# ScalarE instead of VectorE reads the banks of the queries' transposed sums and of the samples' indexer products

## The chip, the core and the metric

The kernel runs on one core of a Trainium2 chip. The metric is the device time of one execution in microseconds, the median of several executions. The core's engines are TensorE (PE), VectorE (DVE), ScalarE (ACT), GpSimd (POOL) and SyncE (SP, which issues most DMAs).

## The reference

One inference step of a decoder layer, for a prompt of 1024 tokens and 8 samples that each add one token to 1024 cached ones, with 1024 features, all in fp32:

```
h    = rms_norm(x) * (1 + scale) + shift          # from the condition c
q, k, v, qi, ki, wi, ga, u, gp = split(h @ w_in)
q, k = rms_norm per head of 64                    # 8 heads, 2 for keys
score = sum over 8 heads of wi * relu(qi . ki)    # the indexer
attend over the 256 tokens of highest score       # per query, causal
p_out = pooled windows (2, 4, 8, 16) of u, times w_pool
y = x + gate * (concat(a_out * silu(ga), p_out * silu(gp)) @ w_out)
```

Two pieces of it matter here. The samples' indexer: for each of the 8 samples the scores of 1024 cached tokens are `sum over heads of wi * relu(qi . ki)`, and the 256 best of 1025 are kept. And the RMS norm of the queries, which needs the sum of squares of every head of every token.

## The kernel before, in words

Each fp32 product is made of three matmuls of fp32r halves, an upper and a lower part of both factors (`hh`, `hl` for the activations, `wh_`, `wl_` for a block of weights). ACT makes the upper part of a weight block (L293), POOL the lower one (L297).

The program has one long stretch in which PE projects blocks of `w_in` one after the other. In the part of interest, from about 200 to 330 us, these are u1, u2, gp0, u3, gp1, q0, gp2, q1, q2 and on, each in three chunks of 344 columns and eight steps of the contraction. In this part the order on PE, DVE and ACT is that in which the program is written. All the smaller work is written as generators that stand in named queues (`beside`); `project` (L514) emits six matmuls, about one microsecond of PE, and then calls `tick`, which lets each queue go on by its rate. So a step that lies one tick later stands six projection matmuls later in PE's order, and behind whatever else the other queues emit in that tick.

`sample_indexer` (L879) is such a generator. For each sample b `pipeline` runs the stages load (POOL's indirect DMA of cached keys, `kin`), turn (PE, L912, `pkin`), copy (ACT, L916, `kidT`), dot (PE, L922, `p_ix`), copy_x (DVE, L927, `sx`), back (PE, L931, `p_ixT`), weigh (DVE, L936 and L939): offsets in ticks of 0, 5, 6, 9, 11, 15 and 16, and a new sample every 4 ticks. The banks of `p_ixT`, of the pooling's products `ppo` (L1223) and of the queries' sums `pqs` and `pqt` are two, in rotation (tag "sm"); `p_ix`, `pkin`, `p_row` and others alternate in two more. A bank is written again once its reader is done.

The weighted sums of heads land in `s_sc`. `sample_search` (L964) then turns them into rows with PE (L973, `p_row`), DVE copies the rows (L975, `s_row`), computes their spread, POOL makes the steps of a bisection from it, and ACT does eight halvings (L734 to L736). In the same stretch `topk` looks for the thresholds of the prompt's blocks: counts by DVE (L764) and ACT (L734), and per halving three small steps of DVE on 128x4: `tk_keep`, `tk_d`, `tk_t` (L768, L770, L772). Later DVE takes the largest (L799) and replaces them (L806); a branch on `tk_bad` (L830), for DVE alone, skips more rounds, and `sample_masks` follows (L1006, L1007, PE's `p_smask` L1011).

For a group of queries `take_q` (L1248) squares the projections on ACT. Its generator `norms` (L1252) sums the squares per head with PE, transposes the sums into the bank `pqt`, DVE copies 16 and 8 of their columns into `qss` (L1266, L1267), and `rstd_steps` forms the reciprocal root: `ms` (DVE, L252), the power `y` (POOL, L253), three steps of DVE (L255 to L257). The pooling's own work on POOL stands in the same queue of POOL as `y`: window sums (L1199), `pdl` (L1215), `sgp` (L1228) and the weights' lower parts.

Of the kernel before, what the change touches and what calls it, by code (L numbers as in the profile page):

```python
# [8 lines left out]
F32 = mybir.dt.float32  # L9
# [20 lines left out]
IXP = 4  # L30
IXB = 15
# [5 lines left out]
AF = mybir.ActivationFunctionType  # L37
ALU = mybir.AluOpType
# [3 lines left out]
P = 128  # L42
# [4 lines left out]
B = 8  # L47
# [9 lines left out]
NPAGES = 8  # L57
CHUNKS = ((0, 344), (344, 344), (688, 344))
QCHUNKS = ((256, 388), (644, 388))
HEADS = 8  # L60
# [5 lines left out]
def kernel(  # L66
# [8 lines left out]
    nc = tc.nc  # L75
# [25 lines left out]
    small = ctx.enter_context(tc.tile_pool(name="small", bufs=2))  # L101
# [5 lines left out]
    def row(name, dt=F32, n=N):  # L107
        return rows.tile([P, n], dt, tag="row", name=name)

    def t2k(name):  # L110
        return work.tile([P, 512], F32, tag="t2k", name=name, bufs=3)

    def s2k(name):
        return work.tile([P, 512], F32, tag="s2k", name=name, bufs=2)

    def page_tile(name, n):
        return work.tile([P, n], F32, tag="pg", name=name, bufs=2)
# [4 lines left out]
    def ps_small(name, shape=(P, 512), dt=F32):  # L122
        return pss.tile(list(shape), dt, tag="sm", name=name)
# [3 lines left out]
    def ps_one(name, shape=(P, 512), dt=F32, tag="sb"):  # L127
        return pss.tile(list(shape), dt, tag=tag, name=name, bufs=1)

    def ps_side(name, shape=(P, 512), dt=F32):  # L130
        side[0] ^= 1
        return ps_one(name, shape, dt, ("sa", "sb")[side[0]])

    def ps_two(name, shape=(P, 512), dt=F32):
        return pss.tile(list(shape), dt, tag="sm", name=name)
# [19 lines left out]
    def beside(queue, gen, rate):  # L155
        queues.setdefault(queue, {"gens": [], "acc": 0.0})["gens"].append((gen, rate))
# [24 lines left out]
    def lag(n):  # L181
        for _ in range(n):
            yield

    def pipeline(n, period, *stages):

        for t in range((n - 1) * period + max(o for o, _ in stages) + 1):
            for o, f in sorted(stages, key=lambda x: -x[0]):
                i, r = divmod(t - o, period)
                if r == 0 and 0 <= i < n:  # L190
                    f(i)
            yield
# [186 lines left out]
    ssq = const.tile([P, NB], F32, name="ssq")  # L379
# [13 lines left out]
    def spread(half, pr):  # L393

        for i in range(4):
            mm(pr[:, i * P:(i + 1) * P], rstd[:, 4 * half + i:4 * half + i + 1].to_broadcast([P, P]), ident,
               start=True, stop=True)
        return scale_rows[:, half * 512:half * 512 + 512], pr
# [52 lines left out]
    to, pr = spread(0, ps_one("pr0", tag="sb"))  # L451
# [23 lines left out]
    to, pr = spread(1, ps_small("pr1"))  # L475
# [395 lines left out]
    def load_pages(dst, src, b):  # L871
        nc.gpsimd.indirect_dma_start(out=dst, out_offset=None, in_=src,
                                     in_offset=bass.IndirectOffsetOnAxis(ap=pidx[:, b:b + 1], axis=0))
# [5 lines left out]
    def sample_indexer():  # L879
        wis_bd = const.tile([B, B, HEADS], F32, name="wis_bd")  # L880
        nc.vector.tensor_tensor(wis_bd, ident[0:B, 0:B].unsqueeze(2).to_broadcast([B, B, HEADS]),
                                wi_s.unsqueeze(1).to_broadcast([B, B, HEADS]), op=ALU.mult)
        pw = ps_side("pwsb", (P, 64))
        mm(pw, ones_f[0:B, :], wis_bd.rearrange("p a b -> p (a b)"), start=True, stop=True)
        yield
        wsb = const.tile([P, 64], F32, name="wsb")
        nc.vector.tensor_copy(wsb, pw)
        nc.vector.memset(s_sc[:, 8, :], NEG)
        yield
        p_ixn = ps_side("p_ixn", (B, B, HEADS))  # L890
        mm(p_ixn.rearrange("p (a o) h -> p a (o h)", o=2), ki_sT, qibd[0:64, :, 0].rearrange("p a o h -> p a (o h)"), start=True, stop=True)
        yield
        rxn = const.tile([B, 64], F32, name="rxn")
        nc.vector.scalar_tensor_tensor(rxn, p_ixn.rearrange("p b h -> p (b h)"), 0.0, wsb[0:B, :],
                                       op0=ALU.max, op1=ALU.mult)
        nc.vector.tensor_reduce(out=s_sc[0:B, 8, :], in_=rxn.rearrange("p (b h) -> p b h", h=HEADS), axis=AX.X,
                                op=ALU.add)
        yield
        nc.gpsimd.affine_select(out=s_sc[0:B, 8, :], in_=s_sc[0:B, 8, :], pattern=[[1, B]],
                                compare_op=ALU.is_equal, fill=NEG, base=0, channel_multiplier=-1)  # L900
        kin, pk, kidT, px, sx, rx = {}, {}, {}, {}, {}, {}

        def load(b):
            if b % 2 == 0:
                kin[b] = page_tile(f"kin{b}", S)
                kin[b + 1] = kin[b][:, 512:S]
            load_pages(kin[b][:, 0:512], rows_ki, b)

        def turn(b):
            pk[b] = ps_side(f"pkin{b}", (P, 4, P))  # L910
            for i in range(4):
                nc.tensor.transpose(pk[b][:, i, :], kin[b][:, i * P:(i + 1) * P], ident)  # L912

        def copy(b):
            kidT[b] = s2k(f"kidT{b}").rearrange("p (g d) -> p g d", d=P)
            nc.scalar.copy(kidT[b], pk[b])  # L916

        def dot(b):

            px[b] = ps_side(f"p_ix{b}", (P, P))  # L920
            for i in range(4):
                mm(px[b][32 * i:32 * i + 32, :], qibd[:, b // 2].rearrange("p g o h -> p (g o h)"), kidT[b][:, i, :],  # L922
                   start=True, stop=True)

        def copy_x(b):
            sx[b] = s2k(f"sx{b}")[:, 0:P]
            nc.vector.tensor_copy(sx[b], px[b])  # L927

        def back(b):
            pt = ps_two(f"p_ixT{b}", (P, NPAGES, 2, HEADS))  # L930
            nc.tensor.transpose(pt.rearrange("p t o h -> p (t o h)"), sx[b], ident)  # L931
            px[b] = pt[:, :, b % 2, :]

        def weigh(b):
            rx[b] = small.tile([P, NPAGES, HEADS], F32, tag="s_rx", name=f"rx{b}")
            nc.vector.scalar_tensor_tensor(  # L936
                rx[b], px[b], 0.0, wsb[:, b * HEADS:(b + 1) * HEADS].unsqueeze(1).to_broadcast([P, NPAGES, HEADS]),
                op0=ALU.max, op1=ALU.mult)
            nc.vector.tensor_reduce(out=s_sc[:, 0:8, b], in_=rx[b], axis=AX.X, op=ALU.add)  # L939

        yield from pipeline(B, IXP, (0, load), (5, turn), (6, copy), (9, dot), (11, copy_x), (IXB, back), (IXB + 1, weigh))


    s_row = {}
# [300 lines left out]
    def take_q(j):  # L1245
        qp[j] = row(f"qp{j}")
        sq = row(f"qsq{j}")

        def norms():
            yield from lag(2)  # L1250

            pq = ps_two(f"pqs{j}", (P, 2, P))  # L1252
            for b in range(NB):
                g, i = divmod(b, 4)
                mm(pq[32 * i:32 * i + 32, g, :], blk[:, 48:80], sq[:, b * P:(b + 1) * P], start=True, stop=True)
            yield
            qs = t2k(f"qs{j}")[:, 0:2 * P].rearrange("p (g t) -> p g t", t=P)
            nc.scalar.copy(qs, pq)
            yield from lag(QLAG)
            pr = ps_two(f"pqt{j}", (P, 24, 16))  # L1260
            for g in range(2):
                nc.tensor.transpose(pr[:, 8 * g:8 * g + 8, :].rearrange("p a b -> p (a b)"), qs[:, g, :], ident)
            mm(pr[:, 16, 0:8], blk, sq[:, S:N], start=True, stop=True)
            yield
            ssq = small.tile([P, 24], F32, tag="qss", name=f"qss{j}", bufs=1)
            nc.vector.tensor_copy(ssq[:, 0:16], pr[:, 0:16, 0])  # L1266
            nc.vector.tensor_copy(ssq[:, 16:24], pr[:, 16, 0:8])  # L1267
            rs = small.tile([P, 24], F32, tag="qrs", name=f"qrs{j}")
            yield from rstd_steps(rs, ssq, 64)
            nc.vector.tensor_scalar(rq8[:, j].rearrange("p a b -> p (a b)"), rs[:, 0:16], 0.125, None, op0=ALU.mult)  # L1270
            nc.vector.tensor_tensor(qbd[0:64, :, j], qp[j][0:64, S:N], rs[0:64, 16:24], op=ALU.mult)
            nc.vector.tensor_tensor(qbd[64:128, :, 4 + j], qp[j][64:128, S:N], rs[64:128, 16:24], op=ALU.mult)

        def take(ci, c0, n, pt):
            nc.scalar.activation(qp[j][:, c0:c0 + n], pt, AF.Copy, scale=qnw)
            nc.scalar.activation(sq[:, c0:c0 + n], pt, AF.Square)
            if ci == 2:
                beside("prep", norms(), 1.0)
        return take
# [490 lines left out]
```

## Time and profile before

| what | value |
|---|---|
| median of 3 runs | 626.29 us (624.5 to 626.4) |
| the profiled execution, its own time | 625.83 us |
| its span in the profile | 624.1 us |
| mean granted clock of PE | 0.997 |
| PE busy | 596.9 us, 96% of the span |
| DVE busy | 386.9 us, 62% |
| ACT busy | 306.7 us, 49% |
| POOL busy | 238.5 us, 38% |

A row of the timeline is an instruction: its start in us, its length in us, engine, line of the program, operation, what it writes and reads (names without their numbers), shapes, and, in brackets, how long its engine had been idle before and what ended that. Where an engine is never idle for long, as PE here, its waits are what can be taken away. A wait of a matmul for a reader of its bank is listed with that reader's engine and line.

### The profile page before, as it was taken

To read this page: it belongs to the slowest core of one execution; us is meant where nothing else is said; L and a number is where in the kernel's file an instruction comes from. 1 tells how busy PE (TensorE), PEld (TensorE's weight loads), DVE (VectorE), ACT (ScalarE), POOL (GpSimd) and SP (SyncE) were. 2 spreads that over 40 slices of the span, in tenths; PEclk is the share of its full clock that TensorE was granted. 3 is DMA by queue.
4 is the path that set the end of the run, shared out by engine and by line. 5 is a ranking of instruction groups with operands and counts; after the bars stand their busy time and mean duration, and the time that the engine had idled before them with its cause. 6 is when DMAs were issued, how large, how long until landed. Compare 5 with 4: busy or idle time off the path is not lost. (4 is left out here: it accounts for less than half of the span.)

```text
span 624.1 us, 10765 instructions
## 1 busy us (share of the span) xinstructions
PE 596.9 (96%) x4086; PEld 492.8 (79%) x4086; DVE 386.9 (62%) x900; ACT 306.7 (49%) x570; POOL 238.5 (38%) x226
## 2 busy tenths in 40 slices
PE   4899999999989998999989999999999999999997
PEld 4678999999979998998868886565666566878876
DVE  4797468647465889959965047555687665464242
ACT  5633554545456885681422458655777554102000
POOL 3111346111247468475816873303544043006000
PEclk9999999999999999999999999999999999999999
DMA  8994122330427123023264243212121136066231
GB/s 307 289 291 102 52 46 76 95 91 19 116 63 222 35 81 90 1 73 79 51 176 136 85 154 136 102 35 69 35 68 35 30 108 227 12 181 206 90 102 67
DMA packets 75290, 66.02 MB, mean 106 GB/s; under 512 B 21828, under 2 KB 63900, under 8 KB 75229
## 3 DMA queue, kind: packets, MB, share of 16 engines
q1 hardware_dynamic: 69731, 50.57, 28.4%
q0 software_dynamic: 3008, 10.49, 5.6%
q10 hardware_dynamic: 2498, 4.27, 1.8%
q8 instruction: 32, 0.52, 0.3%
q14 instruction: 21, 0.17, 0.1%
HBM read 54.44 MB, written 11.10 MB: 105 GB/s over the span
## 5 line engine op out<-in xcount | busy, mean ns | idle before, releaser
L1591 ACT ACTIVATE pr<-pr,mx,rq 128x128 f32<-128x128 f32 (+7 forms) x64 | 55.4, 866 | 12.3 <-DVE mx L1589 11.8
L677 DVE SCALAR_TENSOR_TENSOR sc<-r,wtok,sc 128x512 f32<-128x512 f32 (+5 forms) x42 | 45.1, 1082 | 25.9 <-ACT r L670 24.8
L670 ACT ACTIVATE r<-pi 128x512 f32<-128x512 f32 (+5 forms) x48 | 36.3, 759 | 49.0 <-PE pi L668 43.4
L1619 PE MATMUL po<-pTs,v_sb 128*64 128x256 f32 (+1 forms) x320 | 52.6, 381 | 0.0
L1703 PE MATMUL py<-woh,mh 128*128 128x512 f32 (+1 forms) x136 | 52.1, 383 | 0.0
L1703 PE MATMUL py<-woh,ml 128*128 128x512 f32 (+1 forms) x136 | 51.8, 381 | 0.0
L1703 PE MATMUL py<-wol,mh 128*128 128x512 f32 (+1 forms) x136 | 51.8, 381 | 0.0
L1603 PE MATMUL pT<-ident,pr 128*128 128x128 f32 x288 | 48.8, 283 | 0.1
L1585 DVE CUSTOM_DVE_ANT_0 pr<-pl,amask 128x384 f32<-128x384 f32 (+5 forms) x48 | 42.1, 886 | 9.3 <-PE pl L1582 8.9
L1603 PEld LDWEIGHTS pT<-ident,pr 128*128 128x128 f32 x288 | 32.5, 141 | 17.5 <-issue 15.6
L145 ACT COPY pTs<-pT 128x512 f32<-128x512 f32 x40 | 23.2, 581 | 33.6 <-PE pT L1603 33.6
L1723 DVE TENSOR_TENSOR y<-py,gate_p 128x512 f32<-128x512 f32 (+1 forms) x17 | 11.2, 657 | 42.4 <-PE py L1703 42.4
L1446 POOL TENSOR_TENSOR wol<-wo,woh 128x1024 fp32r<-128x1024 f32 x8 | 19.5, 2444 | 36.6 <-ACT woh L1445 30.3
L147 DVE COPY pTs<-pT 128x512 f32<-128x512 f32 (+1 forms) x40 | 23.3, 582 | 15.1 <-PE pT L1603 11.7
L514 PE MATMUL pj_u<-hh,wh_u 128*128 128x344 f32 x96 | 32.5, 339 | 0.1
L514 PE MATMUL pj_q<-hh,wh_q 128*128 128x344 f32 x96 | 31.8, 331 | 0.0
L514 PE MATMUL pj_gp<-hh,wh_gp 128*128 128x344 f32 x96 | 31.7, 330 | 0.0
L1619 PEld LDWEIGHTS po<-pTs,v_sb 128*64 128x64 f32 x320 | 18.0, 135 | 17.4 <-issue 9.4
L514 PE MATMUL pj_q<-hh,wl_q 128*128 128x344 f32 x96 | 30.8, 321 | 0.5 <-POOL wl_q L297 0.5
L514 PE MATMUL pj_ga<-hh,wh_ga 128*128 128x344 f32 x96 | 31.2, 325 | 0.0
L1703 PEld LDWEIGHTS py<-woh,mh 128*128 128x128 f32 x136 | 25.6, 188 | 6.9 <-DVE y L1724 0.8
L514 PE MATMUL pj_ga<-hh,wl_ga 128*128 128x344 f32 x96 | 30.8, 320 | 0.0
(449 smaller groups left out, 1754.2 us busy)
## 6 DMA issues: line engine op xcount, KB each, us to landing
ada<-in_w_ada_dram SPq DMA_DIRECT2D x16, 512.0 KB
x<-in_x_prompt_dram SPq DMA_DIRECT2D x8, 512.0 KB
gate<-in_w_ada_dram SPq DMA_DIRECT2D x8, 512.0 KB
mix<-mix_dram SPq DMA_DIRECT2D x8, 512.0 KB
xr<-in_x_prompt_dram SPq DMA_DIRECT2D x15, 256.0 KB
out_dram<-y ACTq DMA_DIRECT2D x15, 256.0 KB
mix_dram<-sga SPq DMA_DIRECT2D x12, 172.0 KB
mix_dram<-sgp SPq DMA_DIRECT2D x12, 172.0 KB
```

The costliest lines, as they stand in the source:

```text
L145: nc.scalar.copy(out, in_)
L147: nc.vector.tensor_copy(out, in_)
L514: mm(pt[:m, :n], wt[:, k, :m], ht[k][:, c0:c0 + n], start=k == 0 and q == 0, stop=k == KT - 1 and q == 2)
L670: nc.scalar.activation(r[:, 0:L].rearrange("p (c n) -> p c n", c=nh), pt[:, 0:nh, :n], AF.Relu)
L677: nc.vector.scalar_tensor_tensor(sb[:, 0:L], r[:, 0:L], wtok[:, b, h:h + 1], sb[:, 0:L], op0=ALU.mult, op1=ALU.add)
L1446: nc.gpsimd.tensor_tensor(lo, t, hi.bitcast(F32), op=ALU.subtract)
L1585: nc.vector.tensor_tensor_reduce(out=pr[:, 0:L].rearrange("p (c n) -> p c n", c=nh), in0=pt[:, 0:nh, :n], in1=amask[b].rearrange("p (c n) ...
L1591: exps.append(lambda: nc.scalar.activation(pr[:, 0:L], pr[:, 0:L], AF.Exp, scale=sc, bias=mx, accum_out=sums[j, m][:, bq, s:s + 1]))
L1603: nc.tensor.transpose(pt[:, s, bq * P:(bq + 1) * P], probs[j, 2 * m + bq, s][:, k * P:(k + 1) * P], ident)
L1619: mm(po[j, m][64 * s:64 * s + 64, 0, q0:], v_sb[:, k, 64 * s:64 * s + 64], pTs[j, m, k][:, s, q0:], start=k == 0, stop=k == nk - 1)
L1703: mm(pt[:, part], a[k][:, bs], w[:, part], start=k == ks[0] and q == 0, stop=k == ks[-1] and q == 2)
L1723: nc.vector.tensor_tensor(y, pt, gate[:m, cols], op=ALU.mult)
```

## The change

In the samples' search the stage `weigh` is cut in two. Before, one DVE instruction read the products from the bank and formed `max(x, 0) * w` into `rx`; then DVE summed over heads. Now ACT reads the bank with a Relu into `rx` (the stage `above`, offset 16) and, a tick later (offset 17), DVE multiplies `rx` by the weights, in place, and sums. The pipeline of eight samples is a tick longer by this, and `sample_search`, which follows it in its queue, begins a tick later. For the queries' norms the two DVE copies out of `pqt` become two ACT copies. The program's lines behind L934 are moved by 4.

```diff
+        def above(b):
+            rx[b] = small.tile([P, NPAGES, HEADS], F32, tag="s_rx", name=f"rx{b}")
+            nc.scalar.activation(rx[b], px[b], AF.Relu)
+
         def weigh(b):
-            rx[b] = small.tile([P, NPAGES, HEADS], F32, tag="s_rx", name=f"rx{b}")
-            nc.vector.scalar_tensor_tensor(
-                rx[b], px[b], 0.0, wsb[:, b * HEADS:(b + 1) * HEADS].unsqueeze(1).to_broadcast([P, NPAGES, HEADS]),
-                op0=ALU.max, op1=ALU.mult)
+            nc.vector.tensor_tensor(rx[b], rx[b],
+                                    wsb[:, b * HEADS:(b + 1) * HEADS].unsqueeze(1).to_broadcast([P, NPAGES, HEADS]),
+                                    op=ALU.mult)
             nc.vector.tensor_reduce(out=s_sc[:, 0:8, b], in_=rx[b], axis=AX.X, op=ALU.add)
 
-        yield from pipeline(B, IXP, (0, load), (5, turn), (6, copy), (9, dot), (11, copy_x), (IXB, back), (IXB + 1, weigh))
+        yield from pipeline(B, IXP, (0, load), (5, turn), (6, copy), (9, dot), (11, copy_x), (IXB, back), (IXB + 1, above),
+                            (IXB + 2, weigh))
...
             ssq = small.tile([P, 24], F32, tag="qss", name=f"qss{j}", bufs=1)
-            nc.vector.tensor_copy(ssq[:, 0:16], pr[:, 0:16, 0])
-            nc.vector.tensor_copy(ssq[:, 16:24], pr[:, 16, 0:8])
+            nc.scalar.copy(ssq[:, 0:16], pr[:, 0:16, 0])
+            nc.scalar.copy(ssq[:, 16:24], pr[:, 16, 0:8])
```

The order on DVE, before, where the third sample (number 2) is weighed, between `sx3`, the copy of sample 3's products, and `sx4`; L764 are counts of the prompt's thresholds:

```order
L927 COPY sx3_2505<-p_ix3_2462 128x128
L936 SCALAR_TENSOR_TENSOR rx2_2516<-p_ixT2_2503,wsb_2087 128x64
L939 TENSOR_REDUCE s_sc_861<-rx2_2516 128x8
L764 TENSOR_SCALAR junk_2521,tk_cnt_817<-sc_3_1029,tk_t_818 128x512
L764 TENSOR_SCALAR junk_2523,tk_cnt_817<-sc_24_1082,tk_t_818 128x384
L768 TENSOR_TENSOR tk_keep_819<-tk_cnt_817,tk_least_821 128x4
L770 SCALAR_TENSOR_TENSOR tk_d_820<-tk_keep_819,tk_step_827 128x4
L772 TENSOR_TENSOR tk_t_818<-tk_t_818,tk_d_820 128x4
L927 COPY sx4_2562<-p_ix4_2531 128x128
```

The same place on DVE with the change:

```order
L927 COPY sx3_2507<-p_ix3_2464 128x128
L764 TENSOR_SCALAR junk_2522,tk_cnt_817<-sc_3_1029,tk_t_818 128x512
L764 TENSOR_SCALAR junk_2524,tk_cnt_817<-sc_24_1082,tk_t_818 128x384
L939 TENSOR_TENSOR rx2_2518<-rx2_2518,wsb_2087 128x64
L942 TENSOR_REDUCE s_sc_861<-rx2_2518 128x8
L768 TENSOR_TENSOR tk_keep_819<-tk_cnt_817,tk_least_821 128x4
L770 SCALAR_TENSOR_TENSOR tk_d_820<-tk_keep_819,tk_step_827 128x4
L772 TENSOR_TENSOR tk_t_818<-tk_t_818,tk_d_820 128x4
L927 COPY sx4_2565<-p_ix4_2534 128x128
```

The product and its sum have moved behind the two counts and stand directly ahead of keep, d, t and `sx4`.

On ACT the read of the same sample's bank comes in between the cast of the pooled values `pdh0`, a copy of a chunk of u, and the copy `kidT5` of a later sample's keys; before it was as follows without the row L936:

```order
L736 ACTIVATE tk_t_818<-tk_sign_837,tk_t_818,tk_step_827 128x1
L1217 CAST pdh0_2385<-ps0_1_2315 128x1032
L1028 COPY u2_2439<-pj_u20_2440 128x344
L936 ACTIVATE rx2_2518<-p_ixT2_2505 128x64
L916 COPY kidT5_2553<-pkin5_2539 128x512
L734 ACTIVATE sg_2567,tk_cnt_817<-sc_7_1227,tk_t_818 128x1024
```

So the product of DVE now needs what stands behind `pdh0` and the copy of u on ACT.

The third place is on DVE, behind the branch of L830, where the second query group's sums are read. Before:

```order
L1006 TENSOR_SCALAR s_row_2875<-s_row_2875 8x1025
L1007 SCALAR_TENSOR_TENSOR s_m_862<-ident_78,s_row_2875,s_self_877 8x8
L1266 COPY qss1_4272<-pqt1_3627 128x16
L1267 COPY qss1_4272<-pqt1_3627 128x8
L252 TENSOR_SCALAR ms3_4276<-qss1_4272 128x24
L255 TENSOR_TENSOR yt3_4278<-y03_4277 128x24
```

With the change `ms` of that group stands ahead of the branch, behind the last replacements:

```order
L806 MATCH_REPLACE sc_3_1029<-tk_top_833,sc_3_1029 128x512
L806 MATCH_REPLACE sc_24_1082<-tk_top_833,sc_24_1082 128x384
L252 TENSOR_SCALAR ms3_3649<-qss1_3645 128x24
L830 TENSOR_LOAD tk_bad_834
L830 COMPARE_AND_BRANCH
```

The copies of `qss1` are ACT's now, and `ms` has moved from behind the branch and L1006 to a place ahead of both.

## Rows read from the trace of the kernel before

**Rows 1.** The page, part 1: busy time, share of the span and instructions.
```profile
PE 596.9 (96%) x4086; PEld 492.8 (79%) x4086; DVE 386.9 (62%) x900; ACT 306.7 (49%) x570; POOL 238.5 (38%) x226
```

**Rows 2.** The waits of PE: who waited for what: us in total, times, longest.
```profile
PE pg L1518 <- DVE qss L1267: 3.0, 1, 3.0
PE ppo L1223 <- DVE rx L936: 2.0, 1, 2.0
PE ppo L1223 <- DVE qss L1267: 1.9, 1, 1.9
...
PE ppo L1223 <- ACT pt L1226: 1.1, 1, 1.1
```

**Rows 3.** Timeline, last sample and rows, 241 to 250 us.
```profile
241.69 2.35 POOL L297 TENSOR_TENSOR wl_gp<-wr_gp,wh_gp 128x1024 fp32r<-128x1024 f32 x1 [0.63 <-ACT wh_gp L293]
...
242.73 0.22 DVE L936 SCALAR_TENSOR_TENSOR rx<-p_ixT,wsb 128x64 f32<-128x64 f32 x1
...
243.58 0.60 PE L973 MATMUL p_row<-ident,s_sc 128*8 128x128 f32 x4
...
245.34 1.89 POOL L1199 TENSOR_TENSOR ps<-ps 128x1022 f32<-128x1022 f32 x1
...
245.43 1.81 DVE L770 SCALAR_TENSOR_TENSOR tk_d<-tk_keep,tk_step 128x4 f32<-128x4 f32 x1
...
247.28 0.16 DVE L772 TENSOR_TENSOR tk_t<-tk_t,tk_d 128x4 f32<-128x4 f32 x1
...
247.44 1.89 POOL L1199 TENSOR_TENSOR ps<-ps 128x1020 f32<-128x1020 f32 x1
```

**Rows 4.** Timeline, the samples' chain of rows and halvings, 247 to 274 us.
```profile
247.36 2.23 DVE L975 TENSOR_SCALAR s_row<-p_row 8x512 f32<-8x512 f32 x2
...
254.26 1.16 ACT L734 ACTIVATE s_fl<-s_row,s_t 8x1025 bf16<-8x1025 f32 x1 [4.42 <-POOL s_t L984]
...
273.61 1.04 DVE L991 TENSOR_TENSOR s_t<-s_t,s_step 8x1 f32<-8x1 f32 x1 [6.80 <-ACT s_t L736]
```

**Rows 5.** Single tiles: ns min/median/max, first and last start, shapes.
```profile
L609 ACT COPY ki_s<-pkits x1: 196/196/196, 70.0 to 70.0; 8x64 f32<-8x64 f32 x1
...
L881 DVE TENSOR_TENSOR wis_bd<-ident,wi_s x1: 204/204/204, 181.3 to 181.3; 8x64 f32<-8x64 f32 x1
```

**Rows 6.** Timeline, third sample, 215 to 223 us (start, length, instruction).
```profile
215.29 0.22 DVE L936 SCALAR_TENSOR_TENSOR rx<-p_ixT,wsb 128x64 f32<-128x64 f32 x1
...
217.66 0.58 ACT L916 COPY kidT<-pkin 128x512 f32<-128x512 f32 x1
...
218.23 2.42 POOL L1215 TENSOR_TENSOR pdl<-ps,pdh 128x1032 fp32r<-128x1032 f32 x1
...
219.12 0.29 DVE L927 COPY sx<-p_ix 128x128 f32<-128x128 f32 x1 [1.57 <-PE p_ixT L931]
...
220.62 1.88 POOL L1199 TENSOR_TENSOR ps<-u 128x1023 f32<-128x1023 f32 x1
220.90 0.43 PE L922 MATMUL p_ix<-kidT,qibd 128*32 128x128 f32 x8
```

**Rows 7.** Timeline, first query group, 295 to 308 us.
```profile
295.90 1.15 DVE L799 MAX8 tk_top<-sc 128x8 f32<-128x512 f32 x2
...
297.49 4.21 POOL L253 TENSOR_TENSOR y<-ms,nhalf 128x24 f32<-128x24 f32 x1 [8.57 <-DVE ms L252]
...
304.91 2.40 POOL L297 TENSOR_TENSOR wl_q<-wr_q,wh_q 128x1024 fp32r<-128x1024 f32 x1
...
307.36 0.43 PE L514 MATMUL pj_q<-hh,wl_q 128*128 128x344 f32 x1 [0.47 <-POOL wl_q L297]
```

**Rows 8.** Timeline, branch and second query group, 324 to 328 us.
```profile
324.15 0.69 DVE L1006 TENSOR_SCALAR s_row<-s_row 8x1025 f32<-8x1025 f32 x1 [3.79 <-issue]
...
327.05 1.04 PE L1011 MATMUL p_smask<-ident,s_row 8*128 8x8 f32 x8
```

## The prediction

> **What bounds the kernel now.** I read the totals first: TensorE (PE) is busy for 596.9 of 624.1 us [rows 1]; the four others have at least a third of the span to spare. So a saved instruction on VectorE (DVE) or ScalarE (ACT) is worth nothing by itself, and only a wait of PE that goes, or comes, moves the end. Next PE's waits [rows 2]: three of them fall on the two kinds of DVE reads that the change takes off DVE. A matmul `ppo` waits 2.0 us for a bank that the last sample's product still holds, another 1.9 us for the copies of the first query group, and `pg` 3.0 us for those of the second: 7.0 us together, which is the most that the change could give. Then the timeline around each place, to see what stands next behind each wait.
>
> Two things are to be seen there. First, in the sample search, DVE operations whose two large operands both lie in SBUF stand still while GpSimd (POOL) runs a tensor_tensor, and end when POOL's ends: `tk_d` on 128x4 takes 1.81 us, from 245.43 to 247.24, and POOL's L1199 ends at 247.23; the same kind of operation, `tk_t`, takes 0.16 us when it falls between two POOL operations, at 247.28 [rows 3]. The old product, one operand in PSUM, is not held: 0.22 us inside POOL's wl_gp, which runs from 241.69 to 244.04 [rows 3]. The Trainium skill speaks against the change here: "SBUF — State Buffer", section "Who interferes with whom", says that a DVE instruction with two SBUF inputs contends with a POOL instruction that reads SBUF, that the one issued first keeps the shared port to its end, and that one SBUF input does not contend. By that rule every multiply that comes second would be held, by the old form none; the rows agree for tk_d and for the old product. The sum uses the 1.81 us of the row.
>
> Second, the sample search is a serial chain: DVE's two row copies [rows 4], POOL's steps, then ACT's eight halvings from 254.26 on; DVE sits idle for 6.80 us before it can go on from the last one, at 273.61 [rows 4]. PE itself waits 1.1 us for ACT's `pt` in that stretch [rows 2]. What comes late into this chain comes late to all that follows it, PE too.
>
> **The change, part by part.** *ACT's new work.* Eight reads of 128x64 and eight small copies. The trace has no such read by ACT; its copy of 8x64 from PSUM took 0.196 us [rows 5], so at most 16 times that, 3.1 us over the whole program, on an engine that is idle for half of the span. Taken as nothing: where ACT is full, in the chain, none of the sample reads is left, and the query copies come later. If that cover were gone it would be 0.2 us a read.
>
> *DVE's product.* In place of 0.22 us from PSUM a multiply with two SBUF operands, 0.20 us when free (nearest row: `wis_bd`, 8x64, 0.204 us [rows 5]). When it meets a POOL tensor_tensor it takes up to the rest of that one, 1.81 us and more [rows 3]. The bounds for each of the eight are therefore 0.2 and 2.4 us; which holds is decided by where it stands, below.
>
> *Step A, the third sample.* Before, its product stood at 215.29, straight behind `sx3`, with POOL idle [rows 6]. Now DVE must wait for ACT's read, which stands behind the cast and the copy that end where `kidT` began, 217.66 [rows 6]. The read ends at 217.86, the multiply at 218.1, the reduce at 218.35. The three steps keep, d, t come behind it and no longer before POOL's pdl, which starts at 218.23 and lasts 2.42 us [rows 6]. Keep ends with it (220.65), d with the L1199 that follows (222.50), t slips through the gap of 0.2 us before the next L1199, as at 247.28 [rows 3]. Only then comes `sx4`, which before ran at 219.12; it ends at about 222.95. PE's `p_ix` needs it and started at 220.90 [rows 6]: a new wait of **2.1 us** on PE.
>
> *Step B, the last two samples and the row.* All is 2.1 us late. `ppo` no longer waits (-2.0 us). But the multiplies of samples 6 and 7 now each take a place between two POOL operations. The last one, after the counts at about 245.1, is held by wl_gp (241.69 to 244.04 before, so up to 246.2 now [rows 3]); with its reduce it ends at 246.7. `p_row`, now six matmuls later in PE's order, would be ready for it at 244.65 and waits until 246.75. By the old clock the same point, `p_row` at 243.58 [rows 3] and six matmuls of 0.16 us, was 244.5: PE is 2.2 us late. On DVE keep, d, t come at 247.9, keep is held by the L1199 that is next (to 249.0), d goes through the gap (249.2), and t, issued at 249.22, comes just behind the start of the following L1199 at 249.18, so it is held to 251.1. The row copies start at 251.4 instead of 247.36 [rows 4]. Call this delay D: **4.0 us**. Bounds: 2.2 if t slips through, as it did before, and 0.3 if no multiply is ever held.
>
> *Step C, the chain.* Row copies, steps and halvings are serial, so the chain ends D later, and PE with it, through `pt`: +4.0.
>
> *Step D, first query group.* The wait of 1.9 us on the copies goes. What is late next is wl_q on POOL. It stands behind the power `y`, which starts when DVE's `ms` is done, at 297.49 [rows 7]. Now `ms` stands ahead of two MAX8 (1.15 us at 295.90 [rows 7]), and two copies less, so it is about 1.2 us earlier; wl_q, which ended at about 307.3 [rows 7], ends at 306.1. PE comes there 1.95 us earlier and waits 1.2 instead of 0.47 us [rows 7]: net **-1.3**.
>
> *Step E, second group.* `pg`'s wait of 3.0 us goes, since ACT copies the sums and DVE's branch (3.79 us without work [rows 8]) no longer stands before. What is late next is `p_smask`, which needs DVE's L1006, behind the branch. PE comes to it twelve matmuls behind `pg`, at about 323.7 + D - 1.3, while `s_row` is done at about 325.5 + D: DVE is not sooner there, as `ms` now stands before the branch. `p_smask`, with 1.04 us [rows 8], ends at 326.6 + D; the same point before was 327.05 + 1.04 and six matmuls, 329.05. So D - 2.45 in all after this step (step D's gain is contained in it).
>
> *The rest.* The reads of the third and fourth query group stand in none of PE's waits [rows 2]. Sum: 4.0 - 2.45 = +1.55. On the profiled execution's 625.8 us that makes **627.4 us**; that execution is 0.5 us under the median of 626.29.
>
> **The rivals.**
> 1. *The step slips through.* D is 2.2, not 4.0: t's issue and POOL's next start are 0.04 us apart in my sum. For it: before, t slipped through just there [rows 3]. 2.2 - 2.45 = -0.25: 625.6 us.
> 2. *Nothing is held.* The multiply is a broadcast of 64 columns, and the reads of `wis_bd` [rows 5] were free with POOL quiet; no row shows this form beside POOL. If D is 0.3, the change gives 0.3 - 2.45: 623.7 us. Against it: `tk_d` has two SBUF operands as well and was held to the end of POOL's operation [rows 3]. If also no late branch or wl_q remains, the whole 7.0 us of [rows 2] would come, 618.8 us; two sure successors speak against that.
> 3. *Slower: t is held too at the third sample.* If t misses the gap at 222.5, the next L1199 (1.89 us as in [rows 3]) holds it until 224.6; `sx4` ends at 224.9, `p_ix` waits 4.0 us, and all after it is late by that: D about 6, 6.0 - 2.45 = +3.5: 629.3 us. It decides if t comes more than 0.2 us behind the end of d's POOL operation. Against it: in the gap of the same kind it slipped through [rows 3].
> 4. *The product does not move.* DVE's multiply needs the read by ACT, so it can't stay where it was; but the banks are freed by ACT as said. Under 2 in 100.
>
> **How the numbers follow.** Forecast 0.37 (627.4 us), rival 1 0.25 (625.6), rival 2 0.22 (623.7, a tenth of it the full gain), rival 3 0.16 (629.3). A difference under 0.3%, 1.9 us, can't be told from none; about the median that is 624.4 to 628.2. The forecast's case lies within it but may overrun it; rival 1 lies within it; rival 2 lies just below, rival 3 above. With +-1 us about each: faster 0.27, same 0.44, slower 0.29. The range takes rival 2 and rival 3 with the uncertainty of each and leaves out the full gain and delays past rival 3: 622.2 to 629.8 us.
>
> **What would show it.** Right: in the waits no `ppo` or `pg` on `rx` or `qss`; a new wait of about 2 us of `p_ix` on `sx` near 221, one of `p_row` on `s_sc` near 245, `pj_q` on wl_q over 1 us, `p_smask` on `s_row` about 2 us; single multiplies of 1 us and more among 0.2 us; ACT's first halving of the samples at about 258 instead of 254.26. Wrong: all eight multiplies at 0.2 us (then rival 2), the halvings less than 1 us late, or a wait of PE on the reads of ACT, which I take as none.

## The result and the profile after

The changed kernel takes **629.11 us** (median of 5 runs, 628.75 to 629.93) against 626.29 us (5 runs, 623.87 to 628.23): a ratio of 1.0057, 95% interval 1.0032 to 1.0082, so it is slower by some 0.6%. The profiled execution took 629.93 us, its span is 628.2 us, 4.1 us longer than before. The number lies inside the predicted range, but the case taken for the likeliest (627.4, no change that can be told) is not what came: the loss is two to three times as large. The traces are of one execution each and lie further apart than the medians (2.8 us): in 64 executions beside the experiments the kernel before took 623.2 to 629.4 us, mostly the longer the lower its mean granted clock (1.00 down to 0.986), while the five of the change all stood at 0.988 or 0.989.

Busy times answer to [rows 1]: no engine has much more work, PE has 3.1 us more with the same 4086 matmuls.

```profile
PE 600.0 (96%) x4086; PEld 496.2 (79%) x4086; DVE 392.5 (62%) x892; ACT 309.4 (49%) x586; POOL 240.1 (38%) x226
```

The waits of PE after the change, against [rows 2]: the three waits of 7.0 us on `rx` and `qss` are all gone, as the change means them to be. In their place stand a wait of 4.4 us on `sx`, one of 2.0 on the last sample's sum, 0.7 of the masks, and the wait for `pt` has grown from 1.1 to 3.0 us.

```profile
PE p_ix L922 <- DVE sx L927: 4.4, 1, 4.4
PE ppo L1227 <- ACT pt L1230: 3.0, 1, 3.0
PE p_row L977 <- DVE s_sc L942: 2.0, 1, 2.0
...
PE p_smask L1015 <- DVE s_row L1010: 0.7, 1, 0.7
```

The timeline of the third sample (start, length, instruction) answers to [rows 6]. DVE is idle for 2.25 us until ACT has read the bank; then its multiply, two operands in SBUF, takes 4.70 us instead of 0.22. It goes through all of POOL's pdl and of the window sum that follows it (to 222.43), keep takes another 1.87 us beside the next window sum, and only then `sx` is copied, at 224.87; before it was at 219.12.

```profile
217.57 0.22 ACT L936 ACTIVATE rx<-p_ixT 128x64 f32<-128x64 f32 x1
...
217.82 4.70 DVE L939 TENSOR_TENSOR rx<-rx,wsb 128x64 f32<-128x64 f32 x1 [2.25 <-ACT rx L936]
218.14 2.45 POOL L1219 TENSOR_TENSOR pdl<-ps,pdh 128x1032 fp32r<-128x1032 f32 x1
...
220.55 1.88 POOL L1203 TENSOR_TENSOR ps<-u 128x1023 f32<-128x1023 f32 x1
...
222.65 1.89 POOL L1203 TENSOR_TENSOR ps<-ps 128x1022 f32<-128x1022 f32 x1
222.69 1.87 DVE L768 TENSOR_TENSOR tk_keep<-tk_cnt,tk_least 128x4 f32<-128x4 f32 x1
...
224.79 0.17 DVE L772 TENSOR_TENSOR tk_t<-tk_t,tk_d 128x4 f32<-128x4 f32 x1
224.87 0.28 DVE L927 COPY sx<-p_ix 128x128 f32<-128x128 f32 x1
...
225.30 0.42 PE L922 MATMUL p_ix<-kidT,qibd 128*32 128x128 f32 x8 [4.42 <-DVE sx L927]
```

What is not in the prediction's sum comes right behind this wait. The view by stretches (start:end, length, then busy us and count of PE, PEld, DVE, ACT, POOL; the first of the last three numbers is PE's granted clock) shows the clock at 1.00 before and during the wait, and near half of it in the 4 us after it:

```profile
218.00:220.90 2.90, 2.87 (x19) 2.57 (x17) 2.90 (x1) 2.83 (x6) 2.88 (x3) 1.00 0.59 175
220.90:225.30 4.40, 0.00 (x1) 0.03 (x2) 4.30 (x7) 1.56 (x7) 3.69 (x4) 1.00 0.01 4
225.30:227.30 2.00, 2.00 (x16) 1.80 (x17) 1.97 (x7) 0.59 (x1) 0.00 (x0) 0.65 0.04 8
227.30:229.40 2.10, 2.10 (x9) 2.10 (x8) 1.17 (x4) 0.00 (x0) 0.00 (x0) 0.52 0.00 0
229.40:231.00 1.60, 1.60 (x13) 1.58 (x12) 0.98 (x5) 1.20 (x3) 0.00 (x0) 1.00 0.00 0
...
274.40:277.40 3.00, 0.00 (x0) 0.00 (x0) 0.21 (x1) 2.93 (x8) 0.00 (x0) 0.95 0.28 51
277.40:280.40 3.00, 2.97 (x10) 2.98 (x11) 0.00 (x0) 2.93 (x7) 2.87 (x2) 0.50 0.17 59
```

That is the lower of PE's two levels, 1.2 instead of 2.4 GHz. The last two lines are the wait for `pt` and the 3 us behind it, where the same happens.

The last sample, the row and the chain, against [rows 3, 4], and the places of [rows 8]:

```profile
247.79 2.35 POOL L297 TENSOR_TENSOR wl_gp<-wr_gp,wh_gp 128x1024 fp32r<-128x1024 f32 x1 [0.66 <-ACT wh_gp L293]
...
248.99 1.24 DVE L939 TENSOR_TENSOR rx<-rx,wsb 128x64 f32<-128x64 f32 x1
...
250.54 0.60 PE L977 MATMUL p_row<-ident,s_sc 128*8 128x128 f32 x4 [2.02 <-DVE s_sc L942]
...
253.12 1.86 DVE L772 TENSOR_TENSOR tk_t<-tk_t,tk_d 128x4 f32<-128x4 f32 x1
...
255.22 2.17 DVE L979 TENSOR_SCALAR s_row<-p_row 8x512 f32<-8x512 f32 x2
...
262.07 1.16 ACT L734 ACTIVATE s_fl<-s_row,s_t 8x1025 bf16<-8x1025 f32 x1 [6.21 <-POOL s_t L988]
...
328.73 0.60 PE L1522 MATMUL pg<-ev_g,fold 128*9 128x256 f32 x2
...
332.16 1.04 PE L1015 MATMUL p_smask<-ident,s_row 8*128 8x8 f32 x8 [0.74 <-DVE s_row L1010]
```

With the starts of the same matmuls in both traces the time can be followed along PE:

| matmul | before | after | PE is late by | what was added since |
|---|---|---|---|---|
| `p_ix`, the one that waits | 220.90 | 225.30 | 4.4 | the wait |
| the next `p_ix` | 225.73 | 231.69 | 6.0 | 1.6, the low clock |
| `ppo`, third chunk of gp0 | 243.00 | 246.82 | 3.8 | its wait of 2.0 is gone |
| `ppo` that waits for `pt` | 269.46 | 277.43 | 8.0 | 2.0 of `p_row`, 2.0 of `pt` |
| `ppo` that waited for `qss` | 297.34 | 304.58 | 7.2 | 1.9 gone, low clock added |
| `pg` | 325.39 | 328.73 | 3.3 | 3.0 gone, 0.5 of wl_q gone |
| `pqs` of the third group | 331.07 | 335.23 | 4.2 | 0.7 of `p_smask` |

The last row is the difference of the spans: from there on the two traces run alike.

### The profile page after: what moved, and what is told of

Read it like the earlier page. It is cut to its first block, busy times and chain, and to the rows that moved or that the text cites. A ratio compares the mean times of both kernels' runs of the same rounds, so it can differ in the third digit from the quotient of the medians.

```text
span 628.2 us, 10774 instructions
## 1 busy us (share of the span) xinstructions
PE 600.0 (96%) x4086; PEld 496.2 (79%) x4086; DVE 392.5 (62%) x892; ACT 309.4 (49%) x586; POOL 240.1 (38%) x226
## 5 line engine op out<-in xcount | busy, mean ns | idle before, releaser
L514 PE MATMUL pj_u<-hh,wh_u 128*128 128x344 f32 x96 | 33.9, 353 | 0.1
L514 PE MATMUL pj_u<-hl,wh_u 128*128 128x344 f32 x96 | 31.6, 329 | 0.0
L514 PE MATMUL pj_u<-hh,wl_u 128*128 128x344 f32 x96 | 31.5, 329 | 0.0
L514 PE MATMUL pj_q<-hl,wh_q 128*128 128x344 f32 x96 | 31.1, 324 | 0.0
```

The lines of the kernel that those rows point to most:

```text
L514: mm(pt[:m, :n], wt[:, k, :m], ht[k][:, c0:c0 + n], start=k == 0 and q == 0, stop=k == KT - 1 and q == 2)
```

## The experiments

**Which part loses.** The two parts of the change alone:

```diff
             ssq = small.tile([P, 24], F32, tag="qss", name=f"qss{j}", bufs=1)
-            nc.vector.tensor_copy(ssq[:, 0:16], pr[:, 0:16, 0])
-            nc.vector.tensor_copy(ssq[:, 16:24], pr[:, 16, 0:8])
+            nc.scalar.copy(ssq[:, 0:16], pr[:, 0:16, 0])
+            nc.scalar.copy(ssq[:, 16:24], pr[:, 16, 0:8])
```

> Only the queries' copies are ACT's; the samples stay as before. Theory (the loss is the samples' multiply, held beside POOL, so sx4 and the row are late): no wait of p_ix on sx, none of p_row on s_sc; halvings begin at about 254 us as before; the query places give what they gave in the sum, 1.2 to 3 us: 623 to 625 us. Rival (the loss is in the query part: ms ahead of the branch, y ahead of other work of POOL): 628 us or more with p_smask or pj_q waiting over 2 us.

Measured 624.25 us, ratio 0.9977 (0.9960 to 0.9993): faster. The halvings begin at 253.21, no wait of `p_ix` or `p_row`. Of the waits on `qss` none is left; a wait of 2.4 us on wl_q and one of 1.3 on `qs` are new. The counterpart, the samples' part of the diff alone with DVE's copies of `qss`:

> Only the samples' part of the change. Theory: the 4.4 us wait of p_ix, the wait of p_row of 2 us and the late halvings (about 262 us) stay as in the change, and the reads of qss by DVE come on top: 630 to 634 us. Rival (the loss is in the query part): 626 us or less, like the kernel before.

Measured 631.38 us, ratio 1.0082 (1.0054 to 1.0109). The same 4.4, 3.0 and 2.0 us of waits, halvings at 261.64. So the query part gains a little, and the samples' part loses all and more.

**The multiply's operands.** ACT's Relu writes into an unused piece of the same bank; DVE multiplies from there:

```diff
+            up[b] = pf[:, P:P + 64].rearrange("p (t h) -> p t h", h=HEADS)
...
         def above(b):
-            rx[b] = small.tile([P, NPAGES, HEADS], F32, tag="s_rx", name=f"rx{b}")
-            nc.scalar.activation(rx[b], px[b], AF.Relu)
+            nc.scalar.activation(up[b], px[b], AF.Relu)
...
-            nc.vector.tensor_tensor(rx[b], rx[b],
+            rx[b] = small.tile([P, NPAGES, HEADS], F32, tag="s_rx", name=f"rx{b}")
+            nc.vector.tensor_tensor(rx[b], up[b],
```

> As the change, but ACT's Relu writes into the free half of the same bank, so DVE's multiply has one operand in PSUM; it still waits for ACT. Theory (two SBUF operands beside POOL are held): all eight multiplies near 0.2 us; of the third sample only keep and d are held, sx4 ends near 223, p_ix waits about 2 us instead of 4.4; 625 to 628 us. Rival (the wait for ACT's read is the cost, whatever the operands): p_ix waits 4 us or more and the time is 628.5 us or more.

Measured 628.28 us (twelve executions, 625.6 to 629.3; the trace is of one of 629.29), ratio 1.0027 (1.0005 to 1.0048), between the two ranges expected. With such a spread the wait in the trace says more than the time. Timeline of this kernel at the third sample:

```profile
217.63 0.22 DVE L941 TENSOR_TENSOR rx<-p_ixT,wsb 128x64 f32<-128x64 f32 x1 [2.23 <-ACT p_ixT L937]
...
217.96 2.43 POOL L1221 TENSOR_TENSOR pdl<-ps,pdh 128x1032 fp32r<-128x1032 f32 x1
218.03 4.24 DVE L768 TENSOR_TENSOR tk_keep<-tk_cnt,tk_least 128x4 f32<-128x4 f32 x1
...
220.36 1.88 POOL L1205 TENSOR_TENSOR ps<-u 128x1023 f32<-128x1023 f32 x1
...
222.50 1.86 DVE L772 TENSOR_TENSOR tk_t<-tk_t,tk_d 128x4 f32<-128x4 f32 x1
...
224.71 0.43 PE L922 MATMUL p_ix<-kidT,qibd 128*32 128x128 f32 x8 [4.01 <-DVE sx L927]
```

The multiply from PSUM is free at 0.22 us, at the place where the one from SBUF took 4.70: the operands do decide. But little is won by it, if anything (the interval of its ratio overlaps that of the change): the next step with two SBUF operands, keep, is now the one that stands through both POOL operations, and `p_ix` waits 4.0 us. My theory, that the held multiply carries the loss, fell here. What remained is that DVE's wait for ACT's read carries the whole group (multiply, keep, d, t) from a time in which POOL is idle into one in which it is not; the first step there with two SBUF operands is held.

**One sample of eight.** The third sample alone weighed from PSUM, a tick later, ACT's read of it left out:

```diff
         def above(b):
+            if b == 2:
+                return
...
         def weigh(b):
-            nc.vector.tensor_tensor(rx[b], rx[b],
-                                    wsb[:, b * HEADS:(b + 1) * HEADS].unsqueeze(1).to_broadcast([P, NPAGES, HEADS]),
-                                    op=ALU.mult)
+            w = wsb[:, b * HEADS:(b + 1) * HEADS].unsqueeze(1).to_broadcast([P, NPAGES, HEADS])
+            if b == 2:
+                rx[b] = small.tile([P, NPAGES, HEADS], F32, tag="s_rx", name=f"rx{b}")
+                nc.vector.scalar_tensor_tensor(rx[b], px[b], 0.0, w, op0=ALU.max, op1=ALU.mult)
+            else:
+                nc.vector.tensor_tensor(rx[b], rx[b], w, op=ALU.mult)
```

> As the change, but the third sample alone is weighed as before, by one DVE instruction from PSUM, a tick later. Theory (the one multiply of 4.7 us at the third sample, and what follows its 4.4 us wait of PE, carry the loss): no wait of p_ix on sx, granted clock 1.0 in 220 to 230 us, 623.5 to 626 us. Rival (every multiply and read costs a little, an eighth each): 628 us or more.

Measured 623.80 us, ratio 0.9964 (0.9946 to 0.9983), no wait of `p_ix` on `sx`. One sample of eight makes the difference between slower and faster: 5.3 us.

To keep the two SBUF operands and take away only DVE's wait, the third sample is turned back and read a tick earlier, ahead of the cast `pdh0` on ACT:

```diff
-        yield from pipeline(B, IXP, (0, load), (5, turn), (6, copy), (9, dot), (11, copy_x), (IXB, back), (IXB + 1, above),
-                            (IXB + 2, weigh))
+        def back_above(b):
+            back(b)
+            above(b)
+
+        def early(f):
+            return lambda b: f(b) if b == 2 else None
+
+        def others(f):
+            return lambda b: f(b) if b != 2 else None
+
+        yield from pipeline(B, IXP, (0, load), (5, turn), (6, copy), (9, dot), (11, copy_x), (IXB - 1, early(back_above)), (IXB, others(back)), (IXB + 1, others(above)), (IXB + 2, weigh))
```

> As the change, but the third sample's turn back and ACT's read of it come a tick or more earlier, ahead of the cast pdh0 on ACT; its multiply keeps two SBUF operands and its place on DVE. New theory (DVE's 2.2 us wait for this read pushes multiply, keep, d, t under POOL's pdl and the window sum): no idle time of DVE before the multiply, 0.2 us for it, sx4 in time, no wait of p_ix: 623 to 625 us, as with that sample weighed from PSUM (623.8). Rival (two SBUF operands at this place are enough, whenever the read comes): the multiply of 4 us or more stays and with it p_ix's wait, 628 us or more.

Measured 623.27 us, ratio 0.9971 (0.9948 to 0.9993). The third multiply takes 0.22 us with no idle time before it, and keep, d, t 0.15, 0.16, 0.16 us; `p_ix`'s wait there is gone. One of 1.1 us comes at the next `p_ix`: there the fourth sample's multiply waits 2.5 us for its own read by ACT and is then held for 1.44 us. The third sample:

```profile
212.71 0.22 DVE L939 TENSOR_TENSOR rx<-rx,wsb 128x64 f32<-128x64 f32 x1
...
213.11 0.15 DVE L768 TENSOR_TENSOR tk_keep<-tk_cnt,tk_least 128x4 f32<-128x4 f32 x1
```

So at the third sample neither the two operands nor the read by ACT alone lose anything; DVE's wait for the late read, followed by POOL's work, does. The last sample's multiply is still held beside wl_gp, and `p_row` waits 2.0 us for it, in this kernel too.

**What ends a held instruction.** In the prediction keep got through where one POOL operation follows the other. In the change the multiply did not, at 220.59. A POOL copy of 128x2 (overwritten later) is put between the two:

```diff
             nxt = row(f"ps{g}_{d}")
+            if g == 1 and d == 1:
+                nc.gpsimd.tensor_copy(nxt[:, 0:2], cur[:, 0:2])
```

> As the change, plus one POOL copy of 128x2 between pdl and the window sum that follows it at once; the copy is written over. If a held DVE instruction gets through where POOL turns to an instruction with one input: the multiply ends with pdl near 220.6, 2.8 us long instead of 4.7, and p_ix's wait falls to between 2 and 4 us. If what holds it does not end there: 4.7 to 4.9 us, and 4.4 us or more of wait.

```profile
217.18 2.84 DVE L939 TENSOR_TENSOR rx<-rx,wsb 128x64 f32<-128x64 f32 x1 [2.25 <-ACT rx L936]
217.49 2.43 POOL L1221 TENSOR_TENSOR pdl<-ps,pdh 128x1032 fp32r<-128x1032 f32 x1
...
219.88 0.17 POOL L1204 COPY ps<-u 128x2 f32<-128x2 f32 x1
```

The multiply took 2.84 us, as was expected, to the point: it gets out during the copy. The expected fall of `p_ix`'s wait was a miss: 4.3 us in the single execution that there is of it (628.83 us). The reduce stands between multiply and keep, so keep comes at 220.19, 0.05 us behind the start of the window sum, and is held for 1.86 us; d gets through in the next gap (0.17 us at 222.08); t comes 0.04 us too late at 222.28 and is held for 1.87 us.

An attempt to have POOL idle at this place did not do so:

```diff
         nc.scalar.copy(hi, cur)
-        yield
+        yield from lag(6 if g == 0 else 1)
         nc.gpsimd.tensor_tensor(lo, cur, hi.bitcast(F32), op=ALU.subtract)
```

> As the change, but POOL's subtraction pdl of the first pooling group and all behind it in that queue come about five ticks later, so POOL has no tensor_tensor at 218 to 222 us; DVE still waits for ACT's read. New theory with the shared port: multiply, keep, d, t take 0.2 us each, sx4 is done before 219.5 and p_ix does not wait (the whole time may move for other reasons: POOL's later work). Rival (the wait for ACT alone makes sx4 late, the port has no part): p_ix waits 2 us or more.

POOL's order is not the program's; pdl still ran straight behind its cast, at 215.86 in that trace, the multiply took 4.69 us and `p_ix` waited 4.5. The 636.77 us of its single execution have to do with later work of POOL that the edit did move (PE waits there for wl_gp, wl_q and 4.3 us for the masks). On the question it tells nothing beyond the same long multiply once more.

**A better kernel, and what the reads are worth.** The third and the last sample from PSUM, as above with `b in (2, 7)`:

> As the change, but the third and the last sample are weighed as before, from PSUM, a tick later. Theory: no p_ix wait; no p_row wait (2.0 us, the last multiply beside wl_gp), but ppo waits 2 us for that bank again; the row starts at its old time, so ppo waits 1.1 us less for pt than with the third alone: 622.5 to 624 us. Rival (the last sample's ACT read pays by freeing the bank for ppo): 624.5 to 626 us.

Measured **620.67 us**, ratio 0.9918 (0.9888 to 0.9948), better than expected and faster than both kernels. PE's waits of it:

```profile
PE ppo L1232 <- DVE rx L944: 2.3, 1, 2.3
...
PE ppo L1232 <- ACT pt L1235: 1.3, 1, 1.3
...
PE p_smask L1020 <- DVE s_row L1015: 1.2, 1, 1.2
```

The waits are no shorter than with the third sample alone (there 2.0 on `p_row`, 1.5 on `pt`, 0.9 on `p_smask`). What differs is the clock: with the third alone it fell after the waits of `p_row` and `p_smask` (0.50 in 245 to 247 us, 0.76 in 324.4 to 328), here it stays at 1.00 in all of 200 to 420 us. Two falls at the 1.3 to 1.6 us that they cost in the change make about 3 us, an estimate, which is the 3.1 us between these two kernels. The other executions fit: the mean granted clock was 0.988 to 0.992 in all twelve with the third alone, 0.997 in six of seven here. A part of the gain over the kernel before is clock as well: where that one was granted 0.997 too, it took 623.2 to 625.5 us, most of the time some 3 us more than this kernel, not the 4.8 of the medians. Then all eight from PSUM, a tick later than before, with the queries' copies on ACT:

```diff
-        yield from pipeline(B, IXP, (0, load), (5, turn), (6, copy), (9, dot), (11, copy_x), (IXB, back), (IXB + 1, weigh))
+        yield from pipeline(B, IXP, (0, load), (5, turn), (6, copy), (9, dot), (11, copy_x), (IXB, back), (IXB + 2, weigh))
```

> No sample is read by ACT: all eight are weighed as before, from PSUM, but a tick later, and the queries' copies are ACT's. If the six other reads by ACT give nothing, it is like the kernel with the third and the last sample from PSUM (620.7 us): 619.5 to 622 us. If they are worth something by freeing banks sooner: 622.5 us or more, with waits of PE on rx at more places than the last sample.

Measured 621.02 us, ratio 0.9917 (0.9886 to 0.9948): the same as with six reads by ACT, within the noise. Those reads give nothing that can be told. And the tick alone, with DVE's copies of `qss`:

> The kernel before with the weighing a tick later and nothing else. Theory (the gain is the queries' copies by ACT; the tick only moves their neighbours): the waits on qss of 1.9 and 3.0 us stay, 624 to 627 us. Rival (the shift by a tick is what gains): 621 to 622.5 us.

Measured 622.85 us, ratio 0.9961 (0.9941 to 0.9981): between the two expectations. The waits on `qss` did not stay, though DVE still makes the copies: the first fell from 1.9 to 0.3 us, the second, of 3.0 us, is gone (its copies come at 318.85, ahead of the branch). The first:

```profile
293.81 0.15 DVE L1266 COPY qss<-pqt 128x16 f32<-128x16 f32 x1
...
294.17 1.15 DVE L799 MAX8 tk_top<-sc 128x8 f32<-128x512 f32 x2
294.19 0.40 PE L1223 MATMUL ppo<-pdh,wph 128*128 128x344 f32 x1 [0.25 <-DVE qss L1267]
```

The tick puts the copies ahead of two MAX8 that stood before them [rows 7]. So a good part of what I had put down to ACT's copies is the new place on DVE that comes with the tick; ACT's copies add 1.8 us to that (622.85 to 621.02); in the traces the largest difference is `p_smask`, which waits 1.9 us with DVE's copies, followed by a clock of 0.69 in 324 to 328 us, and 1.0 us with ACT's, at full clock.

## Why the prediction was wrong, point by point

- *What bounds the kernel*: right. The three waits of 7.0 us went, and what counts is which waits of PE took their place.
- *ACT's new work*: right. The reads took 0.208 to 0.230 us, the copies 0.17; no wait of PE on them.
- *Step A*: the step that failed. That ACT's read comes late (217.57 to 217.79, sum 217.86), and that keep and `sx4` then fall behind POOL's work, was right. Wrong was "the multiply at 218.1" and "Keep ends with it (220.65)": the multiply was held as well, and it was held through the point where pdl ends and the window sum begins (217.82 to 222.52). The new wait is 4.4 us, not 2.1. The row that the sum leaned on, `tk_d` in [rows 3], ends where a POOL copy follows (247.17, 0.19 us); between pdl and the window sum there is none. Rival 3 had a wait of 4.0 us at this place and 629.3 us, near what came, but by another instruction: it let t miss its gap, and t passed in 0.17 us.
- *The clock*: missing from the sum, the second thing that failed. The wait of 4.4 us is followed by 4 us at half clock (1.6 us lost), that of 3.0 us by some 3 us of it (ten matmuls at 0.29 us each instead of 0.16, 1.3 us).
- *Step B*: right in itself. `ppo` no longer waits, the last multiply is held by wl_gp (1.24 us), `p_row` waits 2.0 us (sum: 2.1), t is held (1.86 us). The row is 7.9 us late instead of 4.0: the 4.0, 2.3 more of step A and 1.6 of the clock.
- *Step C*: right: halvings 7.8 us late, the `ppo` that waits for `pt` 8.0 us.
- *Step D*: the wait of 1.9 us went, the wait for wl_q did not come (1.2 us expected): PE itself was later, so wl_q was in time. With the queries' copies alone, where PE was not late, it came, at 2.4 us.
- *Step E*: `pg`'s wait went; `p_smask` waited 0.7 us instead of about 2, for the same reason. (The step's own times, 323.7 + D - 1.3 and 325.5 + D, make 3.1 us of it, not 2.)
- In sum the late PE hides later waits, so 3.9 us more in steps A to C and 1.3 of the second low clock became 2.6 us more at the end: 4.1 instead of 1.55.
- The rule of the Trainium skill, "SBUF — State Buffer", section "Who interferes with whom", that two SBUF inputs contend with POOL and one, outside DVE's two-port modes, does not, agrees with the runs: 4.70 us with two, 0.22 with one at the same place. My sum had let one step through at each POOL boundary, which the page does not say, and which the traces show at some boundaries and not at others (last section).

## What to carry to other kernels

When a read moves to another engine, look at the queue of that engine in front of it: the old engine may now sit idle for the read, in order, and carry everything behind it into a worse time. Count small steps with two SBUF operands as one group that must fit where POOL has no tensor_tensor, and don't count on the boundary between two of them: here some let a held step out and others did not. And take a wait of PE that is new at more than its length: where it let the clock fall, this cost another 1.3 to 1.6 us.

## What the runs showed of the hardware that was not expected

- Two POOL tensor_tensors in a row can hold one DVE step through both: 4.70 us (2.45 and 1.88, and the start before them), 4.24 us for keep on 128x4. With a POOL copy of 128x2 between them it is 2.84. Yet a copy is not needed everywhere: in the change's own trace five held steps got out where one POOL tensor_tensor follows another without a copy, among them the seventh sample's multiply, with pdl, and two did not. The kernel before already had one that did not: `yt`, DVE's first step of the reciprocal root, was held for 3.06 us through gate_s (POOL's sum of the gate and its bias) and wl_gp. The first three rows are of the change, the last three of the kernel before:

```profile
241.84 2.41 POOL L1219 TENSOR_TENSOR pdl<-ps,pdh 128x1032 fp32r<-128x1032 f32 x1 [2.51 <-ACT pdh L1217]
...
243.26 1.08 DVE L939 TENSOR_TENSOR rx<-rx,wsb 128x64 f32<-128x64 f32 x1
...
244.22 0.93 POOL L1232 TENSOR_TENSOR sgp<-sgp,pt 128x344 f32<-128x344 f32 x1
...
329.74 0.73 POOL L1521 TENSOR_TENSOR gate_s<-gate_s,bg 9x256 f32<-9x256 f32 x1
329.80 3.06 DVE L255 TENSOR_TENSOR yt<-y 128x24 f32<-128x24 f32 x1 [4.34 <-POOL y L253]
...
330.44 2.37 POOL L297 TENSOR_TENSOR wl_gp<-wr_gp,wh_gp 128x1024 fp32r<-128x1024 f32 x1
```

  In the twelve traces, from 180 to 344 us, it goes by the pair of POOL instructions: from pdl to the first window sum (four times) and from gate_s to wl_gp (ten) the step stays held; from pdl to sgp (21), from sgp to a window sum (18) and from a weight's lower part to sgp (19) it gets out every time. Why the pairs differ stays open.
- The held multiply's row begins at 217.82, 0.32 us before pdl's, longer than the 0.22 us that it takes when free; POOL ended an indirect DMA at 218.12. That such a DMA holds it is unlikely: in the kernel before `tk_t` took 0.16 us at 217.39, inside one from 217.26 to 218.22. By these rows the multiply came first and was held all the same, so starts of rows do not tell here which of the two was first; rows of POOL are rough.
- The clock does not fall behind every wait. In the kernel before the waits of 2.0 and 3.05 us were followed by a clock of 1.00; in the change one of 3.05 us, with the third sample alone one of 2.0 us, and with the queries' copies alone one of 2.4 us were followed by half of it. Which waits are followed by a fall was not settled, and one kernel differs in it: the mean granted clock of the kernel before was 0.997 in the traced execution and 0.986 to 1.00 in others. In the view by stretches the kernel before, around `pg`'s wait of 3.05 us, shows it in the third number from the end:

```profile
322.30:325.40 3.10, 0.05 (x2) 0.04 (x2) 1.18 (x5) 0.03 (x1) 0.00 (x0) 1.00 0.06 19
325.40:329.00 3.60, 3.60 (x22) 2.94 (x23) 0.06 (x1) 1.31 (x2) 3.39 (x1) 1.00 0.00 0
```

The clock is 1.00 in the wait and in the 3.6 us behind it.
